# Logits from half the array's rows, and a wider attention schedule, in a hybrid attention and mLSTM block

## The chip, the cores and the metric

The kernel runs on one core of a Trainium2 chip. The metric is the device time of one execution in microseconds; the time before is the median of three runs. A profile is one more execution, recorded instruction by instruction. The core's engines are named as the profile names them: PE is TensorE (matmuls; PEld its weight loads), DVE is VectorE, ACT is ScalarE, POOL is GpSimd and SP is SyncE, which here only issues DMAs.

## The reference

One layer over 1024 tokens with 1024 channels, all in float32. After an RMSNorm, one input projection gives 11,280 columns for two branches:

- **Differential attention**, 8 heads. Each head has two maps (p = 0, 1) with queries and keys of 64 channels each, and one value of 128 channels. Per map: logits = q k / 8 + relative position bias, masked so that a token sees whole chunks of 64 up to its own; softmax; the head's weights are probs0 - lambda * probs1, applied to the value. Then an RMS norm over the 128 channels and a SiLU gate.
- **mLSTM**, 8 heads of 128 channels: a causal convolution of 4 taps and SiLU on q and k, an exponential input gate and a sigmoid forget gate (16 columns of the projection), chunkwise recurrent state, a layer norm per head, a sigmoid output gate and a SiLU gate.

Each branch is projected to 1024 channels (w_pa, w_pm), multiplied by a sigmoid of its own gate columns (ga, gm), the two are added and projected once more (w_out); residual, final RMSNorm.

```python
attn = probs[0] - lam * probs[1]
merged = g_a * (y_a @ w_pa[layer]) + g_m * (y_m @ w_pm[layer])
h = h + merged @ w_out[layer]
```

## The kernel before

**Arithmetic.** Most products are made of float16 pairs: each operand is scaled and split into a high and a low half, and a product is three matmuls, high by high, high by low, low by high (`mm3`, lines 330 to 332; `rows_unit`, lines 359 to 361). The normed input, transposed, lies in SBUF as `X`.

**Units and slots.** The work is cut into units of 256 weight columns: per attention head `aqk` (q and k) and `avz` (value and gate), per mLSTM head `mqk`, `mvo` and, for every second head, `mz`; further `ga`, `gm` (the merge gates), `pa`, `pm` (branch projections) and `wo`. A unit is 32 slots; after a slot the program may put in a step of something else. A slot is three matmuls of 512 columns or six of 256. Weights arrive by DMA on SP's queue (`wt`), are squared on ACT for their scale and split on ACT and DVE (`wp`); the next unit's preparation runs beside this unit's slots.

**Attention** of one head (`attention`, line 798) is cut into pieces: q and r (line 807: logits of query block i for map 0 and map 1), the combination of the two maps and its transpose (part of r, lines 831 and 840), v (line 850: weights times value), and f, o, t, which norm, gate and store. `PLAN_A` gives the slot at which each piece is emitted; every head's 30 pieces run during the 64 slots of the next head's two units. The eighth head runs by `PLAN_C` in the four `ga` units. The mLSTM heads follow in the same way (`PLAN_M`, `PLAN_N`), the last of them by `PLAN_Z` in the four `gm` units.

**The logits.** The q and k of both maps come out of the projection as `hl`, 128 partitions: map 0 in 0 to 63, map 1 in 64 to 127, each with a high and a low half along the free side. DMAs on SP's queue (lines 609 and 611) copy them, so that `Q` has, for one map, the high half in partitions 0 to 63 and the low in 64 to 127, and `K[p]` has map p's keys in both. A logit tile is then two matmuls over all 128 rows for each 512 keys (line 813): four products, low by low among them. The tile `psb` (two PSUM banks, one buffer) takes one map's logits for up to 1024 keys. DVE adds the bias and takes the extreme of each row (line 823), ACT makes the exponential and its sum (line 827), for map 0 with a shift `lnc` that DVE adds (line 826).

**The order of the work.** The order of emission is a priority. Within it, a planner that costs each instruction decides the order on each engine, so an instruction may run later than its slot where the planner expects its inputs later. On the chip each engine then runs its list in order, and waits on semaphores.

**PSUM.** `pp` has three banks for projections, `psb` two for logits, `pmi` two for everything small and for the values of query blocks 4 to 7, `pvp` one for the values of blocks 0 to 3.

**The gates of the mLSTM.** `if_proj` (line 451) makes 16 columns (high and low weights: 32) from all 1024 tokens: 32 matmuls at line 469 whose output has 32 partitions, one after another into the same 32, each 512 tokens wide.

Of the kernel before, what the change touches and what calls it, by code (L numbers as in the profile page):

```python
# [34 lines left out]
RING = 15  # L35
PLAN_A = [(0, 'q0'), (0, 'r0'), (0, 'q1'), (3, 'r1'), (4, 'q2'), (5, 'r2'), (9, 'q3'), (9, 'r3'), (9, 'q4'), (10, 'v0'), (14, 'v1'), (16, 'r4'), (17, 'q5'), (18, 'v2'), (19, 'r5'), (21, 'q6'), (24, 'r6'), (25, 'q7'), (27, 'r7'), (28, 'v3'), (29, 'v4'), (29, 'v5'), (30, 'f0'), (30, 'o0'), (33, 'v6'), (35, 'v7'), (42, 't0'), (43, 'f1'), (44, 'o1'), (55, 't1')]
PLAN_C = [(0, 'q0'), (0, 'r0'), (6, 'q1'), (7, 'r1'), (7, 'q2'), (9, 'r2'), (16, 'q3'), (19, 'r3'), (19, 'q4'), (19, 'r4'), (19, 'v0'), (22, 'v1'), (22, 'v2'), (25, 'q5'), (28, 'r5'), (29, 'q6'), (31, 'v3'), (32, 'v4'), (33, 'r6'), (37, 'q7'), (38, 'f0'), (38, 'r7'), (46, 'o0'), (52, 'v5'), (52, 'v6'), (63, 'v7'), (64, 'f1'), (67, 'o1'), (82, 't1'), (83, 't0')]
# [11 lines left out]
def block_kernel(ctx, tc, x, norm_w, w_in, lam, subln_w, rel_bias, conv_w, conv_b, b_if,  # L49
# [13 lines left out]
    pmi = ctx.enter_context(tc.tile_pool(name="pmi", bufs=2, space=PSUM))  # L63
# [29 lines left out]

    def m_ps():
        return pmi.tile([P, 512], F32, tag="pmi", name=nm("pmi"))
# [309 lines left out]
    lnc = ctile([P, 1], p="lnc")  # L405
    tb_d = dram.tile([H, P * 513], F32, tag="tbd", name="tb_d")

    def tables():
# [13 lines left out]
        v.scalar_tensor_tensor(lnc, nlam, -1.0, nlam, op0=ALU.mult, op1=ALU.max)  # L422
        v.tensor_scalar(lnc, lnc, 1.0, 2.0 ** -5, op0=ALU.max, op1=ALU.mult)
        s.activation(lnc, lnc, AF.Ln)
        v.tensor_scalar(lnc, lnc, -1.0, None, op0=ALU.mult)
# [23 lines left out]
    gif_d = dram.tile([32, S], F32, tag="gifd", name="gif_d")  # L449

    def if_proj():
# [12 lines left out]
        t = R(shape=[32, S], p="gif")  # L464
        for th in range(2):
            gps = m_ps()
            for i in range(KC):
                for k in range(2):
                    te.matmul(gps[:32, :], parts[:, i, :], x_src(i, th)[k], start=(i + k == 0),
                              stop=(i + k == KC))  # L470
# [597 lines left out]
    for units, side, steps in phases:  # L1068
        if side:
            bg.append(lambda side=side: sides.append(side()))  # L1070
# [152 lines left out]
```

## Time and profile before

| | |
|---|---|
| median of three runs | 1428.03 us (1427.54 to 1428.84) |
| the profiled execution | 1430.35 us, span 1428.5 us, granted clock 0.994 |
| PE / DVE / ACT / POOL busy | 1379.5 / 849.0 / 734.3 / 157.7 us |
| DMA | 150.14 MB, 232,585 packets |
| attention heads 0 to 7 | from about 75 to 550 us |
| mLSTM heads, branch projections | from about 550 to 1340 us |

A row of the groups gives the line of the program, the engine and operation, output and inputs by name, partitions by elements, the count, then busy time, the mean of one in ns, and the idle time of the engine before them with what ended it. The rows of a timeline give start, duration, engine, line and operation, and in brackets the idle time and its releaser. PE's matmuls are pipelined: one is on record for longer than it keeps the next from starting.

### The profile page before, as it was taken

How to read it: one execution, taken by the hardware profiler on the slowest of the kernel's cores; microseconds unless marked ns; L12 is line 12 of the kernel's file. 1: busy time of each engine (PE TensorE's matmuls, PEld its weight loads, DVE VectorE, ACT ScalarE, POOL GpSimd, SP SyncE). 2: the span in 40 equal slices, each digit the busy share in tenths (PEclk: the TensorE clock that was granted, in tenths of full speed). 3: DMA queues.
4: the chain of work that ended last, by engine and by line, in shares of the span. 5: the costliest groups of instructions: out<-in, count | busy, mean ns of one | idle time of the engine just before them, and what ended most of it. 6: DMA issues, size and time to landing. Idle time of an engine off the chain costs nothing.

```text
span 1428.5 us, 25046 instructions
## 1 busy us (share of the span) xinstructions
PE 1379.5 (97%) x9650; PEld 914.8 (64%) x9650; DVE 849.0 (59%) x2310; ACT 734.3 (51%) x1533; POOL 157.7 (11%) x215
## 2 busy tenths in 40 slices
PE   5989999999999999999999999999999999999997
PEld 3657575675756754444586687778769675444786
DVE  6267869678696766433436674765866564233633
ACT  7266657566575667732343444443435344644542
POOL 2001010010100001100102010120211200122004
PEclk9999999999999999999999999999999999999999
DMA  6457366473563634544221413221232135434303
GB/s 200 66 131 154 84 109 136 99 141 84 112 135 87 144 87 117 170 157 129 79 75 60 103 41 94 45 89 45 77 86 75 60 90 158 166 106 164 114 16 118
DMA packets 232585, 150.14 MB, mean 105 GB/s; under 512 B 117297, under 2 KB 209730, under 8 KB 232466
## 3 DMA queue, kind: packets, MB, share of 16 engines
q1 hardware_dynamic: 218450, 123.28, 35.1%
q10 hardware_dynamic: 14016, 25.27, 5.2%
q8 instruction: 75, 1.23, 0.4%
q14 instruction: 44, 0.36, 0.1%
HBM read 90.12 MB, written 18.55 MB: 76 GB/s over the span
## 4 chain that ended last, share of the span: by engine, by line
PE 77%; DVE 8%; DMA 5%; ACT 4%; POOL 3%; issue 2%; SPq 0%; POOLq 0%; DVEq 0%; ACTq 0%
PE pp L330 14%; PE pp L332 14%; PE pp L331 14%; PE pp L359 9%; PE pp L360 9%; PE pp L361 9%; PE psb L813 4%; DMA z<-z 3%; DVE z L823 2%; DMA qw<-rows_d 2%; ACT z L827 1%; DVE wp L259 1%; PE psb L909 1%; DVE z L838 1%; ACT z L845 1%
## 5 line engine op out<-in xcount | busy, mean ns | idle before, releaser
L359 PE MATMUL pp<-wp,X 128*128 128x256 f16 x1280 | 350.4, 274 | 0.0
L360 PE MATMUL pp<-wp,X 128*128 128x256 f16 x1280 | 350.3, 274 | 0.0
L361 PE MATMUL pp<-wp,X 128*128 128x256 f16 x1280 | 350.2, 274 | 0.0
L332 PE MATMUL pp<-X,wp 128*128 128x512 f16 x768 | 291.0, 379 | 1.0 <-DVE wp L259 1.0
L330 PE MATMUL pp<-X,wp 128*128 128x512 f16 x768 | 291.5, 380 | 0.3 <-ACT wp L257 0.3
L331 PE MATMUL pp<-X,wp 128*128 128x512 f16 x768 | 291.3, 379 | 0.0
L257 ACT ACTIVATE wp<-wt,sb 128x512 f16<-128x512 f32 x208 | 137.8, 712 | 110.9 <-DVE sb L138 76.2
L332 PEld LDWEIGHTS <-wp 128*128 128x128 f16 x1024 | 100.0, 98 | 119.3 <-DVE wp L259 1.5
L245 ACT ACTIVATE junk<-wt 128x1024 bf16<-128x1024 f32 x112 | 118.1, 1054 | 100.4 <-DMA wt<-in_w_in_dram 88.0
L330 PEld LDWEIGHTS <-wp 128*128 128x128 f16 x1024 | 100.2, 98 | 102.0 <-issue 1.7
L331 PEld LDWEIGHTS <-wp 128*128 128x128 f16 x1024 | 100.1, 98 | 97.2
L259 DVE SCALAR_TENSOR_TENSOR wp<-wt,sb,wp 128x512 f16<-128x512 f32 x208 | 149.9, 760 | 13.9 <-ACT wp L257 12.2
L359 PEld LDWEIGHTS <-X 128*128 128x128 f16 x1280 | 125.8, 98 | 16.5 <-issue 0.4
L360 PEld LDWEIGHTS <-X 128*128 128x128 f16 x1280 | 125.7, 98 | 16.2
L361 PEld LDWEIGHTS <-X 128*128 128x128 f16 x1280 | 125.7, 98 | 15.7
L827 ACT ACTIVATE z<-z,mx 128x256 f32<-128x256 f32 (+7 forms) x128 | 98.7, 771 | 47.5 <-DVE mx L826 27.1
L823 DVE CUSTOM_DVE_ANT_0 z<-psb,BB,negc 128x256 f32<-128x256 f32 (+7 forms) x128 | 104.1, 813 | 14.9 <-PE psb L813 14.8
L332 PE MATMUL pp<-Y,wp 128*128 128x512 f16 x256 | 97.0, 379 | 0.0
L331 PE MATMUL pp<-Y,wp 128*128 128x512 f16 x256 | 97.0, 379 | 0.0
L330 PE MATMUL pp<-Y,wp 128*128 128x512 f16 x256 | 97.0, 379 | 0.0
L650 DVE SCALAR_TENSOR_TENSOR acc<-up,wcol,acc 128x512 f32<-128x512 f32 x96 | 78.0, 828 | 27.0 <-POOL acc L651 24.8
L813 PE MATMUL psb<-K,Q 128*128 128x512 f16 (+3 forms) x384 | 83.3, 325 | 8.8 <-DMA K<-hl 4.5
(251 smaller groups left out, 2015.8 us busy)
## 6 DMA issues: line engine op xcount, KB each, us to landing
wt<-in_w_in_dram SPq DMA_DIRECT2D x128, 256.0 KB
wt<-in_w_in_dram SPq DMA_DIRECT2D x24, 512.0 KB
K<-hl SPq DMA_DIRECT2D x32, 256.0 KB
gate_d<-tg ACTq DMA_DIRECT2D x32, 256.0 KB
xt<-in_x_dram SPq DMA_DIRECT2D x8, 512.0 KB
Q<-hl SPq DMA_DIRECT2D x32, 128.0 KB
wt<-in_w_pa_dram SPq DMA_DIRECT2D x8, 512.0 KB
ft<-gate_d ACTq DMA_DIRECT2D x16, 256.0 KB
```

The source lines that it names most:

```text
L245: s.activation(j, w.wt[k], AF.Square, accum_out=ss[:, k:k + 1])
L257: s.activation(dst[0], src, AF.Copy, scale=w.sb)
L259: v.scalar_tensor_tensor(dst[1], src, w.sb, dst[0], op0=ALU.mult, op1=ALU.subtract)
L330: te.matmul(ps, wh, xh, start=(start and i == 0), stop=False, **kw)
L331: te.matmul(ps, wh, xl, start=False, stop=False, **kw)
L332: te.matmul(ps, wl, xh, start=False, stop=(stop and i == n - 1), **kw)
L359: te.matmul(ps[:, o], xh[:, t], wh, start=i == 0, stop=False)
L360: te.matmul(ps[:, o], xh[:, t], wl, start=False, stop=False)
L361: te.matmul(ps[:, o], xl[:, t], wh, start=False, stop=i == KC - 1)
L813: te.matmul(sp[:, c:e], Q[:, p, i * P:(i + 1) * P], K[p][:, j, c:e], start=(j == 0), stop=(j == 1))
L823: v.tensor_tensor_reduce(z[:, :n], sp[:, :n], bb[:, S - n:], negc, BIG, op0=ALU.add, op1=ALU.min, accum_out=mx)
L827: s.activation(z[:, :n], z[:, :n], AF.Exp, bias=mx, scale=-1.0, accum_out=rr[:, 2 * i + p:2 * i + p + 1])
```

## The change

- **Logits.** `Q` and `K` are the projection's `hl` tiles themselves; the copies are gone. A piece now makes both maps' logits for the same keys, three products for each map, and each matmul reads 64 partitions of each operand. The tile `psb` holds map 0 in one bank and map 1 in the other, up to 512 keys each. Query blocks 0 to 3 have one such piece; blocks 4 to 7 have two (q and r), each for half of the keys, and the extreme of the second starts from that of the first.
- **Softmax.** The shift `lnc` is replaced by a factor `kap` that scales the combined weights when they are split; the row sums of map 0 enter the norm instead of their reciprocals. The combination is a piece of its own, c. Small operations on one column (`negc`, `invc`, `eps` and others) move from DVE to POOL; the reciprocal of `eps` stays on DVE between POOL's steps.
- **Schedule.** A head's plan is 92 slots long and the next one starts after 84. Four `ga` units stand between the attention heads' units, two `gm` units and the first `mqk` after them, so that the stage has 23 units; the later stages have that many fewer. `RING`, the number of large SBUF tiles, goes from 15 to 17. `pmi` becomes two tiles of one bank; in the attention stage one is kept for the values of blocks 4 to 7.
- **Gate products.** The 32 matmuls of `if_proj` go to four groups of 32 output partitions, taken in turn, so that high and low inputs and the two halves of the tokens have each their own; ACT copies 128 x 512 once, a DMA on ACT's queue stores it, and `if_gates` loads six rows of tiles instead of four and adds two more times.

```diff
+PLAN_A = [(0, 'q0'), (3, 'q1'), (6, 'c0'), (7, 'q2'), (10, 'c1'), (12, 'q3'), (14, 'v0'), (16, 'c2'), (18, 'q4'), (20, 'v1'), (21, 'c3'), (22, 'r4'), (26, 'v2'), (27, 'q5'), (30, 'c4'), (31, 'v3'), (33, 'r5'), (38, 'f0'), (39, 'q6'), (40, 'v4'), (40, 'o0'), (41, 'c5'), (45, 'r6'), (48, 't0'), (52, 'v5'), (53, 'q7'), (54, 'c6'), (59, 'r7'), (65, 'v6'), (68, 'c7'), (80, 'v7'), (84, 'f1'), (86, 'o1'), (92, 't1')]
+PERIOD = 84
...
-        t = R(shape=[32, S], p="gif")
-        for th in range(2):
-            gps = m_ps()
-            for i in range(KC):
+        t = R(shape=[P, 512], p="gif")
+        gps = s_ps()[:, :512]
+        for i in range(KC):
+            for th in range(2):
                 for k in range(2):
-                    te.matmul(gps[:32, :], parts[:, i, :], x_src(i, th)[k], start=(i + k == 0),
-                              stop=(i + k == KC))
-                yield
-            s.activation(t[:, HS[th]], gps[:32, :], AF.Copy, scale=sig[:32, :])
-        nc.sync.dma_start(gif_d, t)
+                    o = (th * 2 + k) * 32
+                    te.matmul(gps[o:o + 32, :], parts[:, i, :], x_src(i, th)[k], start=(i == 0), stop=(i == KC - 1))
+        yield
+        s.activation(t, gps, AF.Copy, scale=sig)
+        s.dma_start(gif_d, t)
...
-        Q = R(F16, [P, 2, S], p="Q")
-        K = [R(F16, [P, 2, S], p="K") for _ in range(2)]
-        live["qk", h] = (Q, K, negc, strip)
+        hl = [R(F16, [P, 2, S], p="hl") for _ in range(2)]
+        live["qk", h] = (hl[0], hl[1], negc, strip)
...
-            if done[cb] == 2:
-                for p in range(2):
-                    src = x2[p * 64:p * 64 + 64]
-                    for j in range(2):
-                        if cb == 0:
-                            nc.sync.dma_start(Q[j * 64:j * 64 + 64, p, :], src[:, j, :])
-                        else:
-                            nc.sync.dma_start(K[p][j * 64:j * 64 + 64, :, :], src)
...
-        v.tensor_scalar(eps, sg, 2.0 ** 13, 2.0 ** -50, op0=ALU.mult, op1=ALU.max)
-        v.tensor_tensor(eps, eps, eps, op=ALU.mult)
+        g.tensor_scalar(eps, sg, 2.0 ** 13, 2.0 ** -50, op0=ALU.mult, op1=ALU.max)
         v.reciprocal(eps, eps)
-        v.tensor_scalar(eps, eps, SUB_EPS, None, op0=ALU.mult)
+        g.tensor_tensor(eps, eps, kap, op=ALU.mult)
+        g.tensor_scalar(eps, eps, eps, SUB_EPS, op0=ALU.mult, op1=ALU.mult)
...
+            c, e = (k * n // 2, (k + 1) * n // 2) if i >= 4 else (0, n * (1 - k))
+            if c < e:
+                sp = s_ps()
+                for a, b in ((0, 0), (0, 1), (1, 0)):
+                    for p in range(2):
+                        m = slice(p * 64, p * 64 + 64)
+                        te.matmul(sp[:, p * 512:p * 512 + e - c], Q[m, a, i * P:(i + 1) * P], K[m, b, c:e],
+                                  start=(a + b == 0), stop=(a == 1))
+                for p in range(2):
+                    z, mx = zs[i][p], sm(p="mx", bufs=8)
+                    v.tensor_tensor_reduce(z[:, c:e], sp[:, p * 512:p * 512 + e - c], bb[:, S - n + c:S - n + e], negc,
+                                           mxs[p] if k else BIG, op0=ALU.add, op1=ALU.min, accum_out=mx)
+                    mxs[p] = mx
...
-            s.activation(hl[:, :n], A[:, :n], AF.Copy)
-            v.tensor_tensor(hl[:, n:2 * n], A[:, :n], hl[:, :n], op=ALU.subtract)
+            s.activation(hl[:, :n], A[:, :n], AF.Copy, scale=kap)
+            v.scalar_tensor_tensor(hl[:, n:2 * n], A[:, :n], kap, hl[:, :n], op0=ALU.mult, op1=ALU.subtract)
...
+    first_units = da_units(0)
+    for h in range(1, H):
+        first_units += da_units(h)
+        if h in (1, 3, 4, 6):
+            first_units.append(ga.pop(0))
+    first_units += gm[:2] + ml0[:1]
+    phases = [(first_units, None, 0)]
+    phases.append((pa + ml0[1:], if_gates, 40))
...
+                if side is None:
+                    h, left = divmod(clock - 64, PERIOD)
+                    if left == 0 and 0 <= h < H:
+                        active.append([attention(h, PLAN_A), [x[0] for x in PLAN_A], 0])
+                    clock += 1
```

More of the change, by code (lines that the diff above doesn't have):

```diff
@@ L62, in block_kernel @@
     psb = ctx.enter_context(tc.tile_pool(name="psb", bufs=1, space=PSUM))
-    pmi = ctx.enter_context(tc.tile_pool(name="pmi", bufs=2, space=PSUM))
+    pmi = ctx.enter_context(tc.tile_pool(name="pmi", bufs=1, space=PSUM))
+    pmx = ctx.enter_context(tc.tile_pool(name="pmx", bufs=1, space=PSUM))
     pvp = ctx.enter_context(tc.tile_pool(name="pvp", bufs=1, space=PSUM))
@@ L92, in s_ps, with x_ps @@
         return psb.tile([P, S], F32, tag="psb", name=nm("psb"))
+    turns = [0, True]
+    def x_ps():
+        return pmx.tile([P, 512], F32, tag="pmx", name=nm("pmx"))
     def m_ps():
+        turns[0] ^= 1
+        if turns[0] and turns[1]:
+            return x_ps()
         return pmi.tile([P, 512], F32, tag="pmi", name=nm("pmi"))
@@ L420, in tables @@
         v.tensor_scalar(nlam, nlam, LAMBDA_INIT, None, op0=ALU.subtract)
[L422 to L425, printed above, removed]
+        v.scalar_tensor_tensor(kap, nlam, -1.0, nlam, op0=ALU.mult, op1=ALU.max)
+        v.tensor_scalar(kap, kap, 1.0, 2.0 ** -5, op0=ALU.max, op1=ALU.mult)
+        v.reciprocal(kap, kap)
         yield
@@ L802, in attention, with qk @@
         rr = sm(cols=16, p="rr", bufs=2)
[L803 removed]
         ssq = sm(cols=8, p="ssq", bufs=2)
[L805 to L807 removed]
+        E, AT, ops, zs, mxs = {}, {}, {}, {}, [None, None]
+        def qk(i, k):
             n = (i + 1) * P
[L809 to L829 removed]
@@ L831, in combine @@
+            if k == i // 4:
+                for p in range(2):
+                    z, mx = zs[i][p], mxs[p]
+                    s.activation(z[:, :n], z[:, :n], AF.Exp, bias=mx, scale=-1.0,
+                                 accum_out=rr[:, 2 * i + p:2 * i + p + 1])
+                    E[i, p] = z
+                zs.pop(i)
         def combine(i):
             n = (i + 1) * P
-            v.reciprocal(rc[:, 2 * i:2 * i + 2], rr[:, 2 * i:2 * i + 2])
             nb = sm(p="nbeta")
-            v.scalar_tensor_tensor(nb, rr[:, 2 * i:2 * i + 1], nlam, rc[:, 2 * i + 1:2 * i + 2],
-                                   op0=ALU.mult, op1=ALU.mult)
+            v.reciprocal(nb, rr[:, 2 * i + 1:2 * i + 2])
@@ L882, in attention @@
         fac, on = {}, {}
-        pieces = dict(q=lambda i: qk(i, 0), r=both, v=pv, f=factor_of, o=scaled_of, t=rows_of)
+        pieces = dict(q=lambda i: qk(i, 0), r=lambda i: qk(i, 1), c=weighted, v=pv, f=factor_of, o=scaled_of, t=rows_of)
         for _, name in plan:
@@ L1064, in block_kernel @@
     at = 1
-    sides = []
-    n = 0
+    sides, active = [], []
+    n = clock = 0
     for units, side, steps in phases:
+        turns[1] = side is not None
         if side:
@@ L1099, in block_kernel @@
                 acc += rate if sides else 0.0
+                if side is None:
[3 more added lines that the diff above has]
+                    clock += 1
+                for a in active:
+                    while a[1] and a[1][0] <= a[2]:
+                        a[1].pop(0)
+                        next(a[0], None)
+                    a[2] += 1
+                active[:] = [a for a in active if a[1]]
                 while plan and plan[0] <= at_slot and sides:
@@ L1108, in block_kernel @@
             n += 1
+        while active:
+            for _ in active.pop(0)[0]:
+                pass
         while plan and sides:
```

87 lines of the change are left out of this document (31 added, 56 removed).

## The prediction

> **What bounds the kernel now.** I read the page's head, then busy time by stage, then the chain of waits, then single instructions in order of time.
>
> ```profile
> span 1428.5 us, 25046 instructions
> ```
>
> ```profile
> 75.00:550.00 475.00, 453.63 (x3420) 298.52 (x3421) 353.61 (x1000) 304.91 (x690) 33.80 (x59) 0.99 0.53 114
> 550.00:1300.00 750.00, 748.79 (x4956) 490.81 (x4955) 401.56 (x1074) 337.33 (x646) 93.46 (x100) 1.00 0.33 95
> 152.54:212.46 59.92, 57.16 (x448) 38.45 (x447) 44.94 (x128) 37.58 (x86) 4.62 (x8) 1.00 0.58 113
> ```
>
> The rows of the second fence give a stretch, its length, then busy time of PE, weight loads, DVE, ACT, POOL, the granted clock, and DMA share and rate. TensorE is busy 748.79 of 750 us from 550 on, with nothing to win there but fewer columns. The attention stage, 75 to 550, has 475 - 453.6 = 21.4 us in which no matmul is in flight. But a matmul is on record for longer than the array needs to take the next one, so I go by distances between starts:
>
> ```profile
> 50.21 0.38 PE L330 MATMUL pp<-X,wp 128*128 128x512 f16 x1
> 50.42 0.38 PE L331 MATMUL pp<-X,wp 128*128 128x512 f16 x1
> 50.64 0.38 PE L332 MATMUL pp<-X,wp 128*128 128x512 f16 x1
> 50.95 0.82 PE L469 MATMUL pmi<-X,wifp 128*32 128x512 f16 x3
> ...
> 57.00 1.03 PE L469 MATMUL pmi<-X,wifp 128*32 128x512 f16 x4
> 57.96 0.28 PE L359 MATMUL pp<-wp,X 128*128 128x256 f16 x1
> ...
> 184.85 0.27 PE L359 MATMUL pp<-wp,X 128*128 128x256 f16 x1
> ...
> 187.36 0.27 PE L361 MATMUL pp<-wp,X 128*128 128x256 f16 x1
> ...
> 190.94 0.23 PE L856 MATMUL pmi<-vr,z 128*128 128x128 f16 x1 [1.97 <-DMA z<-z]
> ...
> 191.95 0.22 PE L856 MATMUL pmi<-vr,z 128*128 128x128 f16 x1
> ```
>
> Width 512 costs 0.43/2 = 0.215 us; width 256, 23 steps in 2.51 us, 0.109; width 128, 18 steps in 1.01 us, 0.056. So a matmul costs its columns by 0.416 ns plus 0.0025 us.
>
> One attention period (64 slots of projection and one head) then needs 96 x 0.215 + 192 x 0.109 for projections (41.6), 108 x 0.056 for values (6.0), and for logits 24 x 0.215 and eight each of widths 128, 256, 384 (0.056, 0.109, 0.162): 7.8. Sum 55.4 us.
>
> ```profile
> 51.02 7.01 PE pmi L469 x32
> 152.54 0.72 ACT z L827 x2
> 185.28 5.62 DMA z<-z
> 452.04 0.72 ACT z L827 x2
> ```
>
> These rows of the chain that ended last (start, duration) show the same exponential five periods apart: 299.5/5 = 59.9 us. **So a period loses 4.5 us, and the stage some 30.** The losses' names, from the waits of PE in that stage (us, times, longest):
>
> ```profile
> PE pmi L856 <- DMA z<-z: 10.7, 8, 2.9
> PE psb L813 <- DMA K<-hl: 4.5, 2, 2.6
> PE psb L813 <- DVE mx L823: 3.8, 9, 1.9
> ```
>
> Values wait for the transposed weights (z); logits wait for their one PSUM tile, which DVE frees. The wait at 190.94 is the last value product of a head behind such a transpose.
>
> **The first stall is another thing.** Single instructions of PE, DVE and SP around it:
>
> ```profile
> 34.67 0.81 SPq L433 DMA_DIRECT2D tb_d<-tb  x1
> 69.32 0.35 SPq L585 DMA_DIRECT2D strip<-tb_d  x1
> 73.58 0.27 PE L361 MATMUL pp<-wp,X 128*128 128x256 f16 x1
> 73.74 0.20 DVE L159 TENSOR_TENSOR s<-wss 128x1 bf16<-128x1 f32 x1 [21.36 <-ACT junk L245]
> 78.29 0.42 DVE L565 SCALAR_TENSOR_TENSOR tz<-tz,pp 128x256 f32<-128x256 f32 x1 [0.32 <-ACT tz L564]
> 79.45 0.42 PE L359 MATMUL pp<-wp,X 128*128 128x256 f16 x1
> ```
>
> PE's wait names K<-hl (4.5 above), but DVE had stood 21.4 us behind a weight load that lands near 73.5; the bias table's write is issued at 34.67 and the strip that depends on it only at 69.32. The projection that resumes at 79.45 needs a PSUM tile that DVE frees at 78.3 to 78.7. Take K<-hl away, and PSUM is next, about 1 us earlier.
>
> **The change part by part.**
>
> **Logits from 64 rows.** Before: 8 x 7.8 = 62.4 us. After: each of 12 pieces per head issues three products (high-high, high-low, low-high) for two maps, six matmuls of 64 rows; the widths of the pieces sum to 4608 per head, so 13,824 columns and 36 pairs. If the two maps of a pair run side by side: 8 x (13,824 x 0.416 ns + 36 x 0.0025) = 46.7 us. If one after the other: 93.4. The trace has no such pair. Nearest is the gate product at L469, which uses 32 of 128 columns and still goes at 0.219 (7.01/32): a part of the array is no faster by itself, which says nothing of two parts at once. The maps lie in different partitions (0 to 63, 64 to 127), different array rows and different PSUM banks, and share nothing that a row shows as limiting; I take 46.7, with 93.4 kept as a rival. The eight narrowest triples may wait for two weight loads instead of 0.056: 24 x 0.056 = +1.3. So -14.4.
>
> **Changes of array shape.** From full array to 128*32 the start moves from 50.64 to 50.95: 0.31 instead of 0.215. Back, the fourth of four from 57.00 starts at 57.65 and the next matmul at 57.96: again 0.31. So 0.095 each way. 96 pieces are entered and left: 192 x 0.1 = **+19.2** (bounds: 0 if hidden, 192 x 0.165 = 32 if each waits until the last matmul is out, 0.38 - 0.215).
>
> The Trainium skill, "TensorEngine Tiling (Array Packing)", section Key Properties, says that changing the tiling mode drains the TensorE, and that tiles can load and multiply in parallel; the trace agrees with the first (0.31 against 0.215), no run here shows the second. By both, the sum is the one above; without the drain it would be 19 us lower.
>
> **Transfers removed.** 64 issues of Q and K copies leave SP's queue, which also carries weight loads and transposes. They gain what is counted under the losses.
>
> **Wider schedule.** A head now gets 84 slots and may run 92 beside the next. Units of the stage grow from 16 with attention interleaved to 23; 6 gate units and one q, k unit only move. Their PE work, weight loads, tanh, and their gate stores on ACT's queue are as many as before. PE needs per period 84 x 0.65 + (46.7 + 1.3 + 19.2 + 48.4)/8 = 69 us. DVE had 44.9 of 59.9. It gains eight split reductions, their cost being the fixed part of these rows
>
> ```profile
> L823 DVE CUSTOM_DVE_ANT_0 z<-psb,BB,negc 128x1024 f32<-128x1024 f32 x16 | 20.5, 1280 | 1.7 <-PE psb L813 1.7
> L823 DVE CUSTOM_DVE_ANT_0 z<-psb,BB,negc 128x512 f32<-128x512 f32 x16 | 11.9, 743 | 1.5 <-PE psb L813 1.5
> L823 DVE DVE_READ_ACCUMULATOR2_ANT mx<- 128x1 f32 x128 | 10.6, 83 | 0.0
> L826 DVE TENSOR_SCALAR mx<-mx,lnc 128x1 f32<-128x1 f32 x64 | 13.5, 211 | 0.3
> L838 DVE SCALAR_TENSOR_TENSOR z<-z,nbeta,z 128x1024 f32<-128x1024 f32 x8 | 10.2, 1276 | 0.0
> L845 ACT ACTIVATE z<-z 128x1024 f16<-128x1024 f32 x8 | 8.3, 1043 | 0.0
> L846 DVE TENSOR_TENSOR z<-z,z 128x1024 f16<-128x1024 f32 x8 | 9.8, 1225 | 4.5 <-ACT z L845 4.5
> ```
>
> (2 x 743 - 1280 + 83 = 0.29 each, 2.3 us), loses eight L826 (1.7) and about eight scalar operations of 0.15, and gets 0.6 units' weight split (about 2.5): some 47 of 69, 68% instead of 75%. DVE stays off the path, with more room.
>
> What then waits is the last value product: c7 to v7 are 12 slots, 12 x 0.65 = 7.8 us, while combine, copy, subtract and transpose take 1.28 + 1.04 + 1.23 + 5.62 (the chain's row at 185.28) = 9.2. So about 1.4 us per head is left, and less for v6, whose 11 slots hold other PE work and shorter operands. I take 1.5 us per head, 12 in all, for 32 before (seven periods at 4.5): **-20** (bounds 0 and -32).
>
> The new order has one wait to watch: DVE's reciprocal of eps now waits for POOL. If POOL stands behind the first strip (until 73.5), everything on DVE behind that reciprocal waits too, the PSUM copies of the first units among them. The operations of eps become ready some us before the strip's issue, so I cost it at nothing; uncovered it is up to 20 us, once.
>
> **Gate products in four groups.** 32 x 0.215 = 6.9 us become 1.7 if the four groups run side by side. But PE then comes 5.2 us sooner to the first stall, whose end is set by the weight load near 73.5 and by DVE after it. I book 0 (bounds -5.2 and 0). With K<-hl gone the stall ends about 1 us sooner: **-1**.
>
> **Elsewhere.** The gate step has two more additions and two more loads beside a stage where PE is never short (550 on); nothing. The last gate stage halves to 64 slots; its side plan ends at slot 45 x 8/7 = 51, and the next stage needs the last head's rows 7 slots in: 13 us for a normalisation and a transpose. I allow **+1.5** for that and the stage's seams.
>
> **Sum:** -14.4 + 19.2 - 20 - 1 + 1.5 = -14.7. The profiled execution took 1430.35 us around its span of 1428.5, 2.3 above the median of 1428.03. Its span less 14.7 is 1413.8; taking the same off the median gives **1413.3 us**.
>
> **The rivals.**
>
> *Pairs don't run side by side.* Every 64-row matmul then takes its full 0.416 ns per column: +46.7, 1460 us, **slower**. It decides where the second matmul of a pair starts more than a third of a pass after the first (1413.3 + 0.32 x 46.7 is the old time). For it: no row shows overlap of matmuls on parts of the array. Against: disjoint rows, partitions and banks.
>
> *Weight loads show.* Each pair needs two loads of Q, 0.098 us on record for a load of that size (the next row); in full-array mode they vanish under the pass. If half of one shows in each of 288 pairs: +14, 1427.
>
> ```profile
> L813 PEld LDWEIGHTS <-Q 128*128 128x128 f16 x384 | 37.1, 97 | 59.5 <-issue 23.1
> ```
>
> The Trainium skill, "TensorE: Matmul & The Clock Gate", Part 3, reports 3.07 times for four row tiles; an estimate from that share of the ideal (0.77) for two tiles is 93.4/1.53 = 61 us, near 1427 as well; no run here shows it.
>
> *The losses stay.* Transposes, or the reciprocal behind POOL, cost about what they do now: -1 instead of -20, so 1432. For it: the product waits by the slot plan, and 12 slots are shorter than the chain above. Against: DVE was full without a gap in the first half of a period, and no longer is.
>
> *The change of shape is hidden* behind waits for PSUM that were there anyway: 1394. Against: 0.31 both ways at L469.
>
> **How the numbers follow.** The forecast as summed has 0.50, with 1402 to 1425 of its own; pairs in sequence 0.13; weight loads 0.10; losses stay 0.13; shape change hidden 0.14. Faster and slower are counted beyond 0.2% (2.9 us), about what a measurement can tell here: faster 0.48 + 0.14 + 0.04 + 0.03 = 0.69, same 0.10, slower 0.21. The range 1390 to 1436 leaves out sequence (0.13) and the lower part of the hidden change.
>
> **What would show it.** In the changed profile: the two maps' matmuls of 64 rows starting within some tens of ns of each other, pairs 0.215 apart at width 512; the first after a projection about 0.1 late and the projection after them too; value products idle about 1.5 us per head for z; the heads 69 us apart; the 32 gate matmuls within 2 us and a first stall longer by as much; from 600 us on, PE as full as now. The forecast is wrong if pairs are in sequence, if shape changes cost clearly more or less than 0.1, or if DVE stands behind POOL before 75 us.

## The result and the profile after

The changed kernel takes **1414.97 us** (median of four runs, 1413.77 to 1415.24) beside 1428.14 for the kernel before, run on the same chip: ratio **0.9906**, 95% interval 0.9889 to 0.9923. That is 13.2 us off the time; the forecast was 1413.3.

The head of the page after, and the busy time by stage. A row gives the stretch, its length, the busy time of PE, weight loads, DVE, ACT and POOL, the granted clock, and the DMA share and rate:

```profile
span 1413.3 us, 25346 instructions
```

```profile
75.00:550.00 475.00, 464.63 (x3514) 276.73 (x3513) 326.02 (x909) 297.33 (x658) 60.21 (x130) 0.99 0.39 91
...
620.00:680.00 60.00, 57.02 (x303) 26.85 (x302) 46.60 (x78) 30.79 (x53) 17.46 (x13) 1.00 0.46 131
680.00:1300.00 620.00, 617.61 (x4288) 429.09 (x4287) 352.19 (x977) 269.01 (x537) 84.23 (x87) 1.00 0.32 92
```

In the attention stage PE's gaps fall from 21.4 us to 475 - 464.63 = 10.4. A new gap of 3 us stands between 620 and 680, where the kernel before had PE full.

The waits of PE between 100 and 650 (total us, times, longest), and between 620 and 690:

```profile
PE psb L820 <- DVE mx L824: 6.2, 9, 1.3
...
PE pmx L859 <- DMA z<-z: 0.3, 1, 0.3
```

```profile
PE pmx L174 <- DVE s L168: 3.0, 1, 3.0
```

The wait of value products for transposes, 10.7 us before, is 0.3. The logits still wait for DVE to free their PSUM tile (3.8 before, 6.2 now).

Single instructions of PE (start, duration): a logit piece of width 512 between projections, one of width 128, and the gate products.

```profile
200.83 0.27 PE L370 MATMUL pp<-wp,X 128*128 128x256 f16 x1
201.04 0.82 PE L820 MATMUL psb<-hl,hl 64*128 64x512 f16 x6
201.79 0.28 PE L368 MATMUL pp<-wp,X 128*128 128x256 f16 x1
```

```profile
73.99 0.27 PE L370 MATMUL pp<-wp,X 128*128 128x256 f16 x1
74.19 0.34 PE L820 MATMUL psb<-hl,hl 64*128 64x128 f16 x6
74.47 0.28 PE L368 MATMUL pp<-wp,X 128*128 128x256 f16 x1
```

```profile
51.94 1.91 PE L479 MATMUL psb<-X,wifp 128*32 128x512 f16 x32
53.78 0.28 PE L368 MATMUL pp<-wp,X 128*128 128x256 f16 x1
```

Six matmuls of width 512 hold PE for 201.79 - 201.04 = 0.75 us: three passes of 0.215 and 0.10 for the way back to the full array. The way into the half-array shape costs 201.04 - 200.83 - 0.11 = 0.10, where 0.11 is the plain step of a projection of width 256. At width 128 it is 0.28 (three passes of 0.056 and 0.11). The 32 gate products take 1.84 us instead of 7.0.

**An account of PE's time.** I add up the distances between the starts of successive matmuls and take off the pure cost by the formula of the prediction (columns by 0.416 ns plus 0.0025 us; the few float32 products by their usual distance). The pure cost of everything that is neither a logit nor a gate product is about 1284 us in every kernel here (within 1), so the rest tells where the time went. For logits the body is the time from the first matmul of a piece to the next other matmul; the entry is what the first one came late. In the kernel before, two waits of the first logits lie in the first stall and are counted there.

| us of PE | before | after | |
|---|---|---|---|
| gate products | 7.1 | 1.9 | -5.2 |
| first stall, 50 to 100 us | 7.8 | 6.1 | -1.7 |
| logits, bodies with the way out | 62.4 | 57.7 | -4.7 |
| logits, entries | 12.6 | 17.5 | +4.9 |
| other waits of the attention heads (before 100 to 550, after 100 to 650) | 18.1 | 2.1 | -16.0 |
| elsewhere (up to 50, and all after the heads) | | | +7.0 |
| sum | | | -15.7 |

The spans differ by 15.2; the remaining 0.5 lies ahead of the first matmul and behind the last. The medians differ by 2 us less, because the profiled execution of before (1430.35) was 2.2 above its median and that of after (1415.1) only 0.1.

Bodies and entries of the logits cancel: **the new logits take 75.2 us, the old ones took 75.0.** The gain of the stage is the waits that went.

The rows of stalls hold more than waits. After the first stall PE ran at a granted clock of 0.50 from 80 to 84 us, in the kernel before and in the changed one: in the changed kernel a projection of width 512 then starts up to 0.43 us after the last, instead of 0.215. The two waits of its first stall are 2.67 and 1.38 us; most of the other 2 of the 6.1 us are this lower clock.

### The profile page after: what moved, and what is told of

It reads as the page before. It is cut to its first block, busy times and chain, and to the rows that moved or that the text cites. A ratio compares the mean times of both kernels' runs of the same rounds, so it can differ in the third digit from the quotient of the medians.

```text
span 1413.3 us, 25346 instructions
## 1 busy us (share of the span) xinstructions
PE 1370.6 (97%) x9842; PEld 892.5 (63%) x9842; DVE 857.4 (61%) x2296; ACT 726.4 (51%) x1529; POOL 197.1 (14%) x303
## 4 chain that ended last, share of the span: by engine, by line
PE 41%; issue 4%; DVE 4%; POOL 2%; ACT 1%; DMA 1%; POOLq 0%; SPq 0%; DVEq 0%; ACTq 0%
PE pp L339 7%; PE pp L341 7%; PE pp L340 7%; PE pp L368 5%; PE pp L370 5%; PE pp L369 5%; DVE acc L648 1%; POOL acc L649 1%; PE psb L913 1%; POOL xr L1162 1%; DMA qw<-rows_d 1%; DVE M L791 1%; PE psb L950 0%; PE psb L952 0%; ACT xr L1161 0%
## 5 line engine op out<-in xcount | busy, mean ns | idle before, releaser
L254 ACT ACTIVATE junk<-wt 128x1024 bf16<-128x1024 f32 x112 | 118.1, 1054 | 68.1 <-DMA wt<-in_w_in_dram 53.1
L368 PEld LDWEIGHTS <-X 128*128 128x128 f16 x1280 | 125.2, 98 | 26.8 <-issue 11.5
L648 DVE SCALAR_TENSOR_TENSOR acc<-up,wcol,acc 128x512 f32<-128x512 f32 x96 | 87.3, 925 | 26.1 <-POOL acc L649 24.0
L649 POOL TENSOR_SCALAR acc<-up,wcol,cols 128x512 f32<-128x512 f32 x32 | 38.4, 1204 | 356.0 <-DVE sig L567 177.9
L824 DVE CUSTOM_DVE_ANT_0 z<-psb,BB,negc 128x512 f32<-128x512 f32 (+5 forms) x128 | 71.8, 596 | 1.3 <-PE psb L820 1.1
```

The lines of the kernel that those rows point to most:

```text
L254: s.activation(j, w.wt[k], AF.Square, accum_out=ss[:, k:k + 1])
L368: te.matmul(ps[:, o], xh[:, t], wh, start=i == 0, stop=False)
L648: tap = lambda j: (lambda: v.scalar_tensor_tensor(a, sh(j), wc(j), a, op0=ALU.mult, op1=ALU.add))
L824: v.tensor_tensor_reduce(z[:, c:e], sp[:, p * 512:p * 512 + e - c], bb[:, S - n + c:S - n + e], negc, mxs[p] if k else BIG, op0=ALU.add, o ...
```

## The experiments

Theory, as the prediction has it: the two maps run side by side; a change of array shape costs about 0.1 us each way; the wider schedule takes away the waits for transposes. The rivals: no overlap, no cost of the shape, no gain from the schedule. All edits are to the changed kernel.

**Order of the six matmuls.** Three of map 0, then three of map 1.

```diff
-                for a, b in ((0, 0), (0, 1), (1, 0)):
-                    for p in range(2):
+                for p in range(2):
+                    for a, b in ((0, 0), (0, 1), (1, 0)):
                         m = slice(p * 64, p * 64 + 64)
                         te.matmul(sp[:, p * 512:p * 512 + e - c], Q[m, a, i * P:(i + 1) * P], K[m, b, c:e],
```

> The changed kernel with the six logit matmuls of a piece ordered by map (three of map 0, then three of map 1) instead of in pairs; same instructions, same order otherwise. Theory (matmuls on different row halves run side by side only when they stand next to each other): only one of three passes still overlaps, five passes instead of three, 2/3 of 46.1 us = +31 us: about 1446 us. Rival (the array works off both halves whatever the order within a piece, since weights are loaded ahead): within 3 us of 1415. Rival (the gain of pairs is small, the 3 ns between starts being only when they are recorded): under +10.

Measured: 1414.93 us, span 1413.2. The expected +31 did not come. A piece of the same width (PE):

```profile
195.03 0.27 PE L370 MATMUL pp<-wp,X 128*128 128x256 f16 x1
195.23 0.83 PE L820 MATMUL psb<-hl,hl 64*128 64x512 f16 x6
195.99 0.28 PE L368 MATMUL pp<-wp,X 128*128 128x256 f16 x1
```

Again 0.76 us for six. The next row shows only what had started by 195.40: two matmuls, within 0.01 us of each other.

```profile
195.23 0.40 PE L820 MATMUL psb<-hl,hl 64*128 64x512 f16 x2
```

The built program lists the matmuls map by map in 95 of the 96 pieces, and a matmul doesn't start beside another on the same rows (0.216 us apart in the run with one half, below). So the fourth in the list has started with the first: PE doesn't keep to the order of the list across the two halves, though the description of the kernel before says that each engine runs its list in order. My idea that the overlap needs the alternation is out. That the halves overlap still stands, but this run doesn't show it by itself.

**Both maps from the same rows.**

```diff
-                        m = slice(p * 64, p * 64 + 64)
+                        m = slice(0, 64)
```

> The changed kernel with both maps' logits made from partitions 0 to 63, so that all six matmuls of a piece use the same half of the array; it leaves out that map 1 has queries and keys of its own. Instructions, widths, shapes and order are the same. After the run with the matmuls ordered by map, where the time stayed and starts were still in pairs: theory (two halves of the array work at once, whichever matmul of the queue is next for each): with one half there are six passes instead of three, +46 us: about 1461 us. Rival (pairs only look simultaneous, and a pair costs what one matmul of 64 rows would cost twice): within 5 us of 1415.

Measured: 1455.31 us, span 1453.5. PE:

```profile
209.56 0.27 PE L370 MATMUL pp<-wp,X 128*128 128x256 f16 x1
209.76 1.47 PE L820 MATMUL psb<-hl,hl 64*128 64x512 f16 x6
211.16 0.28 PE L368 MATMUL pp<-wp,X 128*128 128x256 f16 x1
```

Six matmuls on the same 64 rows hold PE 1.40 us: six passes and a way out. The bodies of all logits take 104.2 us instead of 57.7, so working side by side is worth 46.5 us (worked out in the prediction: 46.7). 6 us come back at the entries (17.5 to 11.5), most of them the wait for DVE to free the tile, which falls from 6.2 to 1.6. Side by side is shown.

**Full rows.** One matmul of 128 rows where there was a pair.

```diff
-                    for p in range(2):
-                        m = slice(p * 64, p * 64 + 64)
-                        te.matmul(sp[:, p * 512:p * 512 + e - c], Q[m, a, i * P:(i + 1) * P], K[m, b, c:e],
+                    te.matmul(sp[:, :e - c], Q[:, a, i * P:(i + 1) * P], K[:, b, c:e],
...
-                    v.tensor_tensor_reduce(z[:, c:e], sp[:, p * 512:p * 512 + e - c], bb[:, S - n + c:S - n + e], negc,
+                    v.tensor_tensor_reduce(z[:, c:e], sp[:, :e - c], bb[:, S - n + c:S - n + e], negc,
```

> The changed kernel with each pair of 64-row matmuls replaced by one of 128 rows and the same width, both maps reading the one result; so it leaves out that the two maps have logits of their own. The array streams the same 46.1 us, but never changes shape. Theory (entering the half-array shape costs about 0.18 us and leaving it 0.095, by the changed kernel's trace 17.5 and about 10 us in all): -18 to -24 us, about 1393, with some 0.05 to 0.08 us of wait left at each entry. Rival (the wait at the entry is for DVE to free the logits' PSUM tile, whatever the shape): only the way out is saved, -9, 1406.

Measured: 1393.21 us, span 1391.4: 21.8 less. PE:

```profile
195.04 0.27 PE L370 MATMUL pp<-wp,X 128*128 128x256 f16 x1
195.15 0.81 PE L818 MATMUL psb<-hl,hl 128*128 128x512 f16 x3
195.79 0.27 PE L368 MATMUL pp<-wp,X 128*128 128x256 f16 x1
```

The time from the projection to the first logit is 0.11 (a plain step) and the body 0.64 (three passes). Over all pieces the bodies take 47.0 us and the entries 5.6, against 57.7 and 17.5. So the change of shape costs 10.7 + 11.9 = **22.6 us** in 96 pieces, 0.235 each; the waits for DVE among the entries are 3.6 here and 6.2 in the changed kernel, which leaves some 20 for the shape alone.

**The copies of q and k put back**, from `hl` to memory that nobody reads, on SP's queue.

```diff
+            done[cb] += 1
+            if done[cb] == 2:
+                for p in range(2):
+                    src = x2[p * 64:p * 64 + 64]
+                    for j in range(2):
+                        if cb == 0:
+                            nc.sync.dma_start(spare[0][j * 64:j * 64 + 64, p, :], src[:, j, :])
+                        else:
+                            nc.sync.dma_start(spare[1 + p][j * 64:j * 64 + 64, :, :], src)
```

> The changed kernel with the 64 removed copies of q and k issued again at their old places on SP's queue, to a place in device memory that nobody reads. Theory (the copies weren't what the attention stage lost its time to; the values' waits went because of the wider schedule): 0 to +3 us, 1415 to 1418. Rival (the transposes come in time because SP's queue is shorter): waits of value products for the transposed weights come back, +8 or more, 1423 or later.

Measured: 1415.28 us (1413.90 to 1417.01), ratio to before 0.9908, interval 0.9893 to 0.9923. The copies cost nothing in the new schedule, and the transposes land as fast with them. The DMA view of the stage (75 to 550) has the median from issue to landing, over the transposes of all sizes whose landing is on record; first this run, then the changed kernel:

```profile
spare<-hl SPq DMA_DIRECT2D x29, 256.0 KB, 4.3
...
z<-z SPq DMA_TRANSPOSE x55, 3.1
```

```profile
z<-z SPq DMA_TRANSPOSE x54, 3.1
```

**The logits of before in the new schedule.** Copies to `Q` and `K`, two matmuls of 128 rows for each map (high and low halves stacked); `RING` 18 and one small tile fewer, to fit.

```diff
-                for a, b in ((0, 0), (0, 1), (1, 0)):
-                    for p in range(2):
-                        m = slice(p * 64, p * 64 + 64)
-                        te.matmul(sp[:, p * 512:p * 512 + e - c], Q[m, a, i * P:(i + 1) * P], K[m, b, c:e],
-                                  start=(a + b == 0), stop=(a == 1))
+                for p in range(2):
+                    for j in range(2):
+                        te.matmul(sp[:, p * 512:p * 512 + e - c], Q[:, p, i * P:(i + 1) * P], K[p][:, j, c:e],
+                                  start=(j == 0), stop=(j == 1))
```

> The changed kernel with the old form of the logits: copies of q and k on SP's queue, two matmuls of 128 rows per map and piece, no change of the array's shape; one more large SBUF tile (18), one less of the gates' half tiles (4), for room. Schedule, softmax, gate products as changed. Theory (the new logits are worth nothing, the schedule everything): logits cost 62.4 + some 6 us at the entries instead of 75.2, so -7 us, about 1408, if the three more large tiles a head find room. Rival (the half-array logits carry part of the gain, by freeing SP's queue and SBUF): 1420 or later.

Measured: 1414.20 us (1413.83 to 1415.79), ratio 0.9902, interval 0.9887 to 0.9917: the time of the changed kernel. So the 13 us come without the new logits; the new softmax and the gate products in groups are still in this run. Inside the sum it isn't the same kernel. Bodies and entries of the logits take 72.9 us instead of 75.2, 3.8 of them one wait of the first piece for ACT to take the gate products out of the PSUM tile that the logits share (PE's waits from 50 to 100):

```profile
PE pmi L174 <- DVE s L168: 3.9, 1, 3.9
PE psb L833 <- ACT gif L481: 3.8, 1, 3.8
```

Without that wait the old logits take 69.1 us, 6 less than the new ones, and PE reaches the branch projections at 639.13 us, where the changed kernel does at 643.59. The stall near 670 then takes 7.0 us instead of 3.4, of which 3.9 are the wait and most of the rest is the lower clock behind it. Busy time by stage there, with a granted clock of 0.50:

```profile
670.00:674.00 4.00, 4.00 (x11) 1.37 (x10) 4.00 (x11) 2.93 (x4) 0.00 (x0) 0.50 0.37 131
```

In the changed kernel the clock stayed at 1.00 from 673 to 680, behind a wait of 2.98. So the equal times hide that the new logits are the slower ones in this schedule.

**Heads every 64 slots**, with the four `ga` units behind the heads instead of between them.

```diff
-PERIOD = 84
+PERIOD = 64
...
-        if h in (1, 3, 4, 6):
-            first_units.append(ga.pop(0))
-    first_units += gm[:2] + ml0[:1]
+    first_units += ga + gm[:2] + ml0[:1]
```

> The changed kernel with the next head started every 64 slots instead of 84, and the gate units and the q, k unit after all attention units instead of between them. Theory (the lost time in the stage goes because softmax work is spread over more projection): DVE's share in the stage rises from 69% to about 82%, PE waits for the logits' tile and for transposed weights again, +10 to +20 us, about 1430. Rival (separate pieces for the combination and longer distances within a head do it, the spreading does nothing): within 3 us of 1415.

Measured: 1422.57 us, span 1420.8: 7.6 slower than the changed kernel, under the expected 10 to 20. The attention stage by itself does lose 10: PE reaches the branch projections at 653.63 instead of 643.59 us, and the stall near 670 (below) is missing here. Its waits of PE between 100 and 650:

```profile
PE psb L820 <- DVE mx L824: 16.1, 14, 2.4
```

No wait for transposes comes back in this list; what grows is the wait for DVE to free the logits' tile, 16.1 us instead of 6.2 (entries 26.9 instead of 17.5). So the spacing isn't needed to take the value waits away; that lies in the plan within a head (12 slots from the last combination to the last value, 8 before) or in what it leaves DVE to do, which this run doesn't separate. No run has the old spacing and the copies together. What the wider spacing with gate units between does is to keep DVE from holding up the logits.

**Gate products one group after the other.**

```diff
-        for i in range(KC):
-            for th in range(2):
-                for k in range(2):
+        for th in range(2):
+            for k in range(2):
+                for i in range(KC):
                     o = (th * 2 + k) * 32
```

> The changed kernel with the 32 gate matmuls ordered group by group (eight into the same 32 output partitions, then the next eight), so that no two neighbours use different groups; all else the same. Theory (the 5.2 us that the grouping saves are spent waiting for the weight load at 75 us): the 32 take 6.9 instead of 1.8 us, the wait of 4.3 us goes, the time rises by 0 to 1.5 us (about 1415.5). Rival (the grouping is worth what it saves): +5, 1420.

Measured: 1418.45 us (1418.08 to 1419.30), ratio 0.9927, interval 0.9911 to 0.9944: 3.5 slower than the changed kernel. Its PE:

```profile
51.27 4.54 PE L479 MATMUL psb<-X,wifp 128*32 128x512 f16 x32
55.74 0.28 PE L368 MATMUL pp<-wp,X 128*128 128x256 f16 x1
...
79.92 0.16 PE L174 MATMUL pmi<-s,ones 128*128 128x1 bf16 x1 [2.67 <-DVE s L168]
81.47 0.61 PE L339 MATMUL pp<-X,wp 128*128 128x512 f16 x1 [1.39 <-ACT wp L266]
```

and the same two places in the changed kernel:

```profile
77.97 0.16 PE L174 MATMUL pmi<-s,ones 128*128 128x1 bf16 x1 [2.67 <-DVE s L168]
79.51 0.61 PE L339 MATMUL pp<-X,wp 128*128 128x512 f16 x1 [1.38 <-ACT wp L266]
```

PE leaves the gate products 1.96 us later (55.74 for 53.78) and resumes after the first stall 1.96 later (81.47 for 79.51). The stall, 2.67 and 1.4 both times, moves with PE. Not all of this lasts: at the first branch projection PE is only 0.74 us late (644.33 for 643.59). The rest of the difference comes behind the stall near 670, where the clock of this profile was 0.50 from 676 to 678, so the 3.5 us are not the price of the order alone.

The serial order takes 4.47 us instead of 7: four matmuls start alone, then (from 52.14 us) two within 0.01 us of each other, which must be of two groups, since those of one group start 0.216 apart. The first matmuls of each group fall beside the last four of the group before, so here too PE looked ahead in its list.

**One pool for the small PSUM tiles**, as before the change, against the idea that the turn between two pools makes the new waits after 680.

```diff
-    pmi = ctx.enter_context(tc.tile_pool(name="pmi", bufs=1, space=PSUM))
-    pmx = ctx.enter_context(tc.tile_pool(name="pmx", bufs=1, space=PSUM))
+    pmi = ctx.enter_context(tc.tile_pool(name="pmi", bufs=2, space=PSUM))
...
-                ops[i // 4] = x_ps() if i else v_ps()
+                ops[i // 4] = m_ps() if i else v_ps()
```

> The changed kernel with the two one-bank PSUM tiles that are used in fixed turns put back into one pool of two, from which all take in the order of need. Theory (PE's new waits after 680 us, 5.0 instead of 2.1 us, are for the bank whose turn it is): those 3 us go, about 1412. Rival (they come from DVE's order, not from the turn): within 1.5 us of 1415; and slower if value sums of blocks 4 to 7 then hold both banks in the attention stage.

Measured: 1415.08 us (1414.58 to 1417.17), ratio 0.9905, interval 0.9888 to 0.9921; the waits between 680 and 1300 stay. The pools are not their cause.

**The new stall near 670, and fewer pieces.** In the changed kernel, DVE and PE there:

```profile
668.67 3.87 DVE L510 TENSOR_TENSOR_SCAN m<-ff,gi 8x1024 f32<-8x1024 f32 x1
...
673.11 0.14 DVE L168 TENSOR_TENSOR s<-wss 128x1 bf16<-128x1 f32 x1
```

```profile
673.31 0.16 PE L174 MATMUL pmx<-s,ones 128*128 128x1 bf16 x1 [2.98 <-DVE s L168]
```

PE's small product for the next weights' scale waits for a sum on DVE, which stands behind a scan of the mLSTM gates. The scan in four parts:

```diff
-        v.tensor_tensor_scan(fl(m), fl(lf), fl(gi), 0.0, op0=ALU.add, op1=ALU.max)
-        yield
+        for c in range(0, S, 256):
+            v.tensor_tensor_scan(fl(m)[:, c:c + 256], fl(lf)[:, c:c + 256], fl(gi)[:, c:c + 256],
+                                 fl(m)[:, c - 1:c] if c else 0.0, op0=ALU.add, op1=ALU.max)
+            yield
```

> The changed kernel with the one long scan of the gate step (1024 columns, 3.87 us on DVE) cut into four scans of 256 that hand their last column on; everything else is the same. If the stall of 3 us near 670 us is caused by that scan standing ahead of the sum of the weight scale on DVE, the sum now waits for at most one quarter of it: the stall falls from about 3.4 to about 1 us and the time by 2 to 3 us, to about 1412.5. Rival: the stall ends with something else (the exponential and the weight squares on ACT before it); then the stall stays and the time is 1415 within 1.5.

Measured: 1414.37 us (1413.02 to 1416.36), ratio 0.9901, interval 0.9886 to 0.9915. PE's wait there:

```profile
671.93 0.16 PE L174 MATMUL pmx<-s,ones 128*128 128x1 bf16 x1 [1.64 <-DVE s L168]
```

The wait falls from 2.98 to 1.64, not to a quarter, and the time by less than these runs can tell. DVE shows why:

```profile
668.60 2.27 DVE L511 TENSOR_TENSOR_SCAN m<-ff,gi 8x256 f32<-8x256 f32 x1
...
671.11 0.71 DVE L511 TENSOR_TENSOR_SCAN m<-ff,m,gi 8x256 f32<-8x256 f32 x1
671.75 0.12 DVE L168 TENSOR_TENSOR s<-wss 128x1 bf16<-128x1 f32 x1
```

The sum stands behind two of the four parts, and the first part takes 2.27 us where the later ones take 0.71; why is open. The scan is part of the cause, since the wait followed it (2.6 to 3.1 in the other runs that have the long scan, the new logits and this stall); it wasn't worth 2 to 3 us.

With that, query blocks 0 and 1 of a head share a piece (128 and 256 columns side by side in each bank):

```diff
+            def segments(i, k):
+                n = (i + 1) * P
+                return (k * n // 2, (k + 1) * n // 2) if i >= 4 else (0, n * (1 - k))
...
+            blocks = [i] if k or i > 1 else [0, 1] if i == 0 else []
+            if blocks and segments(blocks[0], k)[0] < segments(blocks[0], k)[1]:
+                sp, o = s_ps(), 0
+                for i in blocks:
...
+                    c, e = segments(i, k)
+                    for a, b in ((0, 0), (0, 1), (1, 0)):
+                        for p in range(2):
+                            m = slice(p * 64, p * 64 + 64)
+                            te.matmul(sp[:, p * 512 + o:p * 512 + o + e - c], Q[m, a, i * P:(i + 1) * P], K[m, b, c:e],
+                                      start=(a + b == 0), stop=(a == 1))
+                    o += e - c
...
```

> As the run with the scan in four, and query blocks 0 and 1 of each head in one piece (widths 128 and 256 side by side in one PSUM tile): 88 pieces instead of 96, so 16 changes of array shape fewer. By entry 0.18 and exit 0.095 us per piece, measured in the changed kernel, 8 x 0.275 = 2.2 us less than the run with the scan alone: about 1410.5, if that one is at 1412.5. Rival: the time lost at the entry of a piece is a wait for the freed PSUM tile and not the shape; then the larger piece keeps the tile longer and the time is the same as that of the run with the scan alone, or up to 2 us longer.

Measured: **1410.35 us** (1409.77 to 1410.55), ratio 0.9870, interval 0.9854 to 0.9887, 4.0 less than with the scan alone where 2.2 were expected. Entries fall by 2.0 us (17.5 to 15.5) and bodies by 1.5 (57.7 to 56.2), 3.5 us where the changes of shape alone were put at 2.2; the rest is elsewhere and within what single profiles differ by. It is faster than both kernels of this case: its interval and that of the changed kernel (0.9889 to 0.9923) don't meet.

Last, the logits of before in the new schedule, with the scan in four and with the gate products in a small PSUM tile of their own:

```diff
-        gps = s_ps()[:, :512]
+        gps = m_ps()
```

> The new schedule with the logits of before over all 128 rows (with the copies, RING 18), now with the gate product in a tile of its own instead of the logits' PSUM tile, and with the scan in four. With the gate product in the logits' tile, the first logits waited 3.8 us for the copy out of it, and the wait near 670 us was 7.0 us. If both go, up to 8 us of the 1414.2 go: about 1407 to 1410, and the logits from 64 rows are not needed for the gain at all. Rival: the first stall ends with the next unit's projection as before and the wait near 670 is set by ACT; then 1413 to 1415.

Measured: 1412.69 us (1410.93 to 1414.19), ratio 0.9887, interval 0.9873 to 0.9902; the hoped-for 1407 to 1410 was missed. PE's waits from 50 to 100:

```profile
PE pmi L174 <- ACT gif L481: 4.3, 1, 4.3
PE psb L835 <- DMA gif_d<-gif: 4.0, 1, 4.0
```

The two waits of the first stall only changed their names (what the second waits for the trace gives as the store of the gates; the copies of K come on another queue at the same time and aren't told apart). Near 670 PE still waits 2.6 us, and the clock behind it is 0.50 from 670 to 672. Between this kernel and the merged one no order is shown: their intervals overlap.

## Why the prediction was right, and where its terms were off

The forecast 1413.3 is 1.7 from the median, inside its own range of 1402 to 1425. The two terms of the logits came out for the reasons given; the others came out in part for other reasons, and their misses cancel. Term by term, on PE's account:

| term | forecast | measured | how |
|---|---|---|---|
| logits from 64 rows | -14.4 | -15.4 | bodies 62.4 to 47.0, the full-rows run's |
| changes of shape | +19.2 | +22.6 | changed kernel less full-rows run |
| waits of the attention heads | -20 | -23.0 | other waits 18.1 to 2.1, entries 12.6 to 5.6 |
| gates and first stall | -1 | -6.9 | -5.2 and -1.7 |
| elsewhere | +1.5 | +7.0 | 0 to 50 +0.9, after the heads +6.1 |
| sum | -14.7 | -15.7 | |

**Logits from 64 rows: right.** The old logits' 62.4 came out to the digit. Pairs are side by side (46.5 us by the run with one half), so the rival of pairs in sequence, 1460, is out; that run landed at 1455. The allowance of 1.3 for narrow pieces was not needed: 0.28 us at width 128 holds nothing beyond passes and way out. The rival of weight loads that show is out too: the six matmuls at 512 leave room for three passes and 0.10. The Trainium skill, "TensorE: Matmul & The Clock Gate", Part 3, from whose four-tile figure I had estimated 61 us, therefore doesn't carry over to two halves: the 57.7 us of bodies less 96 ways out of 0.10 are some 48.

**Changes of shape: right, a little small.** 0.10 in and 0.10 to 0.11 out where nothing else is awaited, as at the gate product before. The 22.6 includes about 2.6 us more waits for DVE. The rival that the shape change is hidden, 1394, is out: the full-rows run, in which it is gone, ended at 1393. The Trainium skill, "TensorEngine Tiling (Array Packing)", Key Properties, has a drain at each change of mode; the run agrees that a change costs time, 0.2 us for both ways.

**Waits of the attention stage: right in sign and size, wrong in one step.** I set a chain of 9.2 us, from the last combination to the last value product, against 12 slots of 7.8, and so left 1.5 us of waiting per head. The step that failed is the 7.8. One head's end in the changed kernel:

```profile
276.65 1.28 DVE L841 SCALAR_TENSOR_TENSOR z<-z,nbeta,z 128x1024 f32<-128x1024 f32 x1
...
280.16 1.27 DVE L849 SCALAR_TENSOR_TENSOR z<-z,kap,z 128x1024 f16<-128x1024 f32 x1
281.50 2.02 SPq L851 DMA_TRANSPOSE z<-z  x1
...
287.63 0.22 PE L859 MATMUL pmx<-vr,z 128*128 128x128 f16 x1
```

The landing of this transpose isn't on record; that of the first head's, of the same size, is:

```profile
L851 SPq DMA_TRANSPOSE z<-z x1: 1838/1838/1838, 140.4 to 140.4; - x1
...
DMA to landing us min/median/max: 4.3/4.3/4.3
```

So the chain is about 281.50 + 4.3 - 276.65 = 9.1, as worked out: the transpose is shorter than the 5.62 of the kernel before, and the steps ahead of it are longer by the gaps between them. But PE comes 11.0 us after the combination, since the slots between also hold other pieces, which I had left out of the 7.8. Nothing is left to wait. The 12 us of waiting that I left in the sum did not come; against that, the logits' entries kept 6.2 us of waits for DVE, which I had counted as gone with the 4.5 per period. The cause I gave, that the removed copies free SP's queue, isn't it: with the copies back the time is the same. And the logits don't earn it, since the kernel with the old ones in this schedule takes the same time. How much of the gain is the plan within a head and how much the new softmax, no run separates. The rival that the losses stay, 1432, is out. DVE's share came out as forecast (326.02 of 475 us, 69%), and the heads follow at (555.6 - 78.7)/7 = 68.1 us, where 69 was worked out, by the copies of the bias strip, one for each head:

```profile
L799 DVE COPY BB<-strip x8: 282/294/295, 78.7 to 555.6; 128x256 f32<-128x256 f32 x8
```

**Gate products and first stall: wrong.** The size was right (1.84 us for 32), the step that failed is "whose end is set by the weight load near 73.5 and by DVE after it", for which I booked 0. It held for the order of before, where DVE stood behind that load with the copies of the unit queued behind it. In the changed kernel the copies come first:

```profile
75.75 0.42 DVE L582 SCALAR_TENSOR_TENSOR vr<-pp,vr 128x256 f16<-128x256 f32 x1 [4.23 <-ACT vr L581]
...
77.75 0.16 DVE L168 TENSOR_TENSOR s<-wss 128x1 bf16<-128x1 f32 x1 [0.61 <-ACT junk L254]
```

DVE waits for PE's results (through ACT), PE finishes its unit, and only then does the weight scale follow. PE resumes at 79.51, as before at 79.45, but with the whole `avz` unit done, where before it had stopped inside it. The run with the groups in sequence shows that the end of the stall moves with PE, 1.96 us for 1.96. At that place the bound of -5.2 was the right value.

**DVE behind POOL: right that it costs nothing.** The reciprocal of `eps` runs long before POOL takes the strip:

```profile
47.08 0.15 DVE L620 RECIPROCAL eps<-eps 128x1 f32<-128x1 f32 x1
```

```profile
74.17 0.49 POOL L598 TENSOR_SCALAR strip<-strip,invc 128x256 f32<-128x256 f32 x1 [26.29 <-DMA strip<-tb_d]
```

**Elsewhere: wrong in place and size.** I allowed 1.5 us for the last gate stage, where nothing came, and "nothing" for the gate step from 550 on, "where PE is never short". 3.4 us came at that step, near 670. Another 2.9 come between 680 and 1300, mostly where state products wait for DVE (rows of PE's waits from 800 to 1200):

```profile
PE pmi L932 <- DVE nb L144: 1.0, 2, 0.5
PE pmx L932 <- DVE nb L144: 0.5, 1, 0.5
```

These stay open: neither the pools nor the copies are their cause, and why DVE comes later there wasn't tried. The stall near 670 differs between profiles by more than its wait, since the clock behind it dropped in some (last section).

So that the forecast came so near is luck in part: -5.9 us at the gates and the first stall that I hadn't booked stand against +5.5 elsewhere that I hadn't either, and the misses of the other three terms (-1.0, +3.4 and -3.0) cancel too.

## What to carry to other kernels

Cost a matmul on part of the array by passes and add the change of shape each time it is entered and left; here, 0.2 us for each of 96 small pieces ate all that fewer products had saved, and eight pieces fewer (with the scan cut) made the fastest version. When a change touches arithmetic and schedule together, put the old arithmetic into the new schedule: here that run gave the whole gain. Equal times can hide unequal parts, so add up PE's time by place, and read the granted clock behind each stall. Before an edit ahead of a stall is booked at nothing, look whether the order on the engine that ends the stall is still the same, since its end may move with the saved time after all.

## What the runs showed of the hardware that was not expected

- Two halves of the array by rows overlap also when all matmuls of the one stand ahead of those of the other in the list: 0.76 us for six of width 512 in either order, 1.40 when all use the same half.
- Four groups of 32 output columns ran 3.8 times as fast as one (1.84 us against 7.0 for 32 matmuls). Queued group by group they still took only 4.47 us, with the start of each group beside the last four matmuls of the group before.
- The cost of a change of array shape hardly depends on the width of the piece: 0.10 us in and 0.10 out at width 512, 0.09 and 0.11 at 128.
- A wait of some 3 us of PE can cost more than itself, and the same wait does not always do so. Near 670 the wait was 2.6 to 3.1 us in the changed kernel and in the runs by map, with full rows, with the groups in sequence, with the copies and with one pool. The clock behind it stayed at 1.00 in the first three and was 0.50 for some 2 us and more in the other three (676 to 678, 675 to 677 and 674 to 676). After 3.9 us, in the run with the logits of before, it was 0.50 for 4 us and more. What decides it these runs don't show.
- The transposes of one head differ in size, and the landing after issue goes with it: 2.3 us for the smallest block, 4.3 for the largest.
